# Two modulation units beside w_out's products, and modulation weights loaded two steps ahead, in a two-layer diffusion block

## The chip, the cores and the metric

The kernel runs on one core of a Trainium2 chip. The metric is the time of one execution on the device in microseconds (us), the median over runs. A core has TensorE (matrix products, called PE in the profile), VectorE (DVE), ScalarE (ACT), GpSimd (POOL) and SyncE (SP, which issues most copies from memory). Each engine works through its own queue in order.

## The reference

Two layers over 512 latent tokens `x` and 256 context tokens `ctx`, each of width 1024, all in float32. Each layer first makes six modulation vectors from a conditioning vector, for the latents and for the context:

```
mod_x = split(silu(c) @ w_mod[i] + b_mod[i], 6)
mod_c = split(silu(c_ctx) @ w_mod[i] + b_mod[i], 6)
...
z = modulate(x, norm1_gain[i], mod_x[0], mod_x[1]) @ w_in[i]
x = x + mod_x[2] * mixer_merge(z, attention, ...)        # ends in a product with w_out
x = x + mod_x[5] * swiglu(modulate(x, norm2_gain[i], mod_x[3], mod_x[4]), w_ffn_in[i], w_ffn_out[i])
```

`mixer_merge` adds three gated branches (pooling, windowed attention, spatial gating) and multiplies by `w_out`. The context goes through the same layer in layer 0 and gives only keys and values in layer 1. The output is the latent stream after a last norm.

## The kernel before, in words

**Products.** Every float32 weight is split in a rounded part (`wh`, ScalarE) and a rest (`wl`, VectorE), activations likewise, and each product is three TensorE passes (lines 334 to 336). A raw weight is copied into one of six buffers named `raw` (pool `rawp`, half a megabyte each); the split reads it, and the buffer is free again.

**Modulation.** The product with `w_mod` has a single row on the left, so it is not done on TensorE. `mod_steps` takes a *unit* of 512 of the 6144 columns: four copies `wm` of two 128-row blocks each, and for each block a multiply-add into the accumulator `mac0` for the latents (line 264, VectorE) and, where the context needs it (all of layer 0, units 0 to 3 of layer 1), a multiply on ScalarE (line 261) and an addition into `mac1` on GpSimd (line 262). Then 16 small TensorE products (`ps_mod`, line 274) sum over partitions, and `take_mod` adds the bias. There is one buffer for each accumulator. The copies `wm` use the same six `raw` buffers as the weights. Units 10 and 11 make `mod_x[5]` and `mod_c[5]`, which are first read by the FFN's evictions (line 1238); units 6 to 9 make `mod_x[3]` and `mod_x[4]`.

**Fillers.** `mod_steps` is a generator. The object `fill` holds such generators, and `fill.tick()`, called at chosen places between TensorE's products, takes each one step further; `fill.drain()` runs them to their end. A unit takes five ticks, and a generator two more. Before, each step loads the copy of the next step. The order on an engine is settled when the kernel is built; program order is its priority, and an instruction whose data and buffers are ready may come before earlier ones.

**Stages, with their times in the profile.** The context's mixer of layer 0 (to about 260 us, with units 4 and 5, a step every five ticks), the latents' mixer of layer 0 (to 702 us, the last 55 of them w_out's products, in which `last_first` does the last three output tiles in two halves of the tokens so that the FFN's norm can begin), the first FFN for both streams (702 to 1240 us), the latents' mixer of layer 1 (to about 1690 us) and the second FFN.

**The first FFN** (`Seven`, `ffn_seven`) forms its up products by a scheme with seven products instead of eight for each pair of hidden tiles. `Seven.pair` makes one pair: `load` copies the two raw weights `raw_g` and `raw_u`, `sums` makes sums of their blocks on VectorE, four items `a` to `d` split them and multiply. Pairs 0 to 2 are "early": `seven.ahead` holds their `load` and the first two of their sums, (3, 1), to be called by hand. Between the pairs, after hidden tiles 3, 6, 10, 14 and 18, stand down products: `chunk` multiplies the last 3 or 4 hidden tiles with `w_ffn_out`, two output tiles to an item, into one of two PSUM buffers, and VectorE evicts them into `X` (line 1238). Units 0 to 3 of layer 1 run there, one tick after each pair's item `d`.

Of the kernel before, what the change touches and what calls it, by code (L numbers as in the profile page):

```python
# [5 lines left out]

# [15 lines left out]
KT = D // P  # L22
# [28 lines left out]
def hybrid_dit_kernel(ctx, tc, I, out):  # L51
# [39 lines left out]
    SX = Stream("x", CTX, SEQ, 0)  # L91
# [144 lines left out]

    def mod_steps(l, u0, u1, stride=1):

        nxt = None

        def load(u, k2):
            raw = rawp.tile([P, 2, 512], F32, tag="raw", name=f"wm{l}{u}{k2}")
            nc.sync.dma_start(raw, I["w_mod"][l, k2 * P:(k2 + 2) * P, u * 512:(u + 1) * 512].rearrange("(k p) n -> p k n", p=P))
            return raw

        for u in range(u0, u1):
            nv = 2 if l == 0 or u < 4 else 1
            acc = [macp.tile([P, 512], F32, tag=f"mac{r}", name=f"mac{l}{u}{r}") for r in range(nv)]
            for k2 in range(0, KT, 2):
                if nxt is None:  # L250
                    nxt = load(u, k2)
                    yield
                raw = nxt
                for r, a in enumerate(acc):
                    for k in range(2):
                        sck = scv[:, k2 + k, r:r + 1]
                        if k2 + k == 0:
                            (G if r else V).tensor_scalar(a, raw[:, k, :], sck, None, ALU.mult)
                        elif r:
                            q = t2(f"mq{l}{u}{k2}{k}")  # L260
                            S.activation(q, raw[:, k, :], AF.Copy, scale=sck)  # L261
                            G.tensor_tensor(a, a, q, ALU.add)  # L262
                        else:
                            V.scalar_tensor_tensor(a, raw[:, k, :], sck, a, ALU.mult, ALU.add)  # L264
                if k2 + 2 < KT or u + 1 < u1:
                    nxt = load(u, k2 + 2) if k2 + 2 < KT else load(u + 1, 0)
                for _ in range(stride):
                    yield
            yield
            ps = pmain(f"ps_mod{l}{u}")[:, :P]  # L270
            for r, a in enumerate(acc):
                av = a.rearrange("p (t j c) -> p j t c", j=4, c=32)
                for j in range(4):
                    T_.matmul(ps[32 * j:32 * j + 32, :].rearrange("p (t c) -> p t c", c=32), pick[:, r, :], av[:, j],
                              start=(r == 0), stop=(r == nv - 1))
            take_mod(l, 4 * u, 4, ps, nv)
# [485 lines left out]
                summed = g, a, w  # L762
            yield

    def mixer(s, l, H, L, mods=None, mid=None, then=None, end=None, done=None, last=None):
        nm0 = f"{l}{s.name}"
        rot = s.r == 0
        per = 2048 // s.T
# [111 lines left out]
            fill.tick()  # L880
        if last is not None:
            last(one, acc)
        fill.drain()
        return acc

    def up_units(l, j, w):
# [138 lines left out]
    class Seven:  # L1025
# [71 lines left out]
        def pair(self, j, A, early=None):  # L1097
# [113 lines left out]
            def run_d(w):  # L1211
                self.product(d["P"], w, 0, "T4", False)
                H, L = A(j)
                for i, (x, y) in enumerate(((d["P"], d["g1"]), (d["m5"], d["m6"]))):
                    V.tensor_tensor(y, x, y, ALU.mult)
                    y3 = y.rearrange("p (b t) -> p b t", t=P)
                    S.activation(blocks(H, i), y3, AF.Copy)
                    V.tensor_tensor(blocks(L, i), y3, blocks(H, i).bitcast(F32), ALU.subtract)
                fill.tick()

            if early is not None:
                self.ahead.append((load, partial(sums, (3, 1))))
# [2 lines left out]
    def ffn_seven(sv, streams, l, finish, mods):  # L1225
        fo = I["w_ffn_out"][l]
        heads = [0, 3, 6, 10, 14, 18]
        A = []

        def hidden(j):  # L1230
            t = (sv.fap if j % 6 < 4 else sv.fbp).tile([P, 2, NT], F32R, tag="fa", name=f"fa{l}{j}")
            A.append([t[:, 0, :], t[:, 1, :]])
            return A[j]

        def down(s, n, w, c0, m, ps):
            gemm(ps, w, m, *[[A[c0 + j][x][:, s.cols] for j in range(m)] for x in range(2)])
            x = X[:, n, s.cols]
            V.scalar_tensor_tensor(x, ps, modv[l][:, 40 + n, s.r:s.r + 1], x, ALU.mult, ALU.add)  # L1238

        def size(c0):  # L1240
            return ([h for h in heads if h > c0] + [NF])[0] - c0

        def chunk(c0):
            m = size(c0)
            for n in range(0, KT, 2):
                def prep(n=n):
                    raw = rawp.tile([P, m, 256], F32, tag="raw", name=f"raw_fo{l}{c0}{n}")
                    nc.sync.dma_start(raw, fo[c0 * P:(c0 + m) * P, n * P:(n + 2) * P].rearrange("(k p) n -> p k n", p=P))
                    return split_unit(raw, m, 256, f"fo{l}{c0}{n}")

                def go(w, n=n):
                    for i in range(2):
                        ps = ps_s.tile([P, 1024], F32, tag="ps", name=f"pfo{l}{c0}{n + i}")
                        for s in streams:
                            o = 512 if s.r else 0
                            down(s, n + i, [x[:, :, i * P:(i + 1) * P] for x in w], c0, m, ps[:, o:o + s.T])

                yield prep, go

        sv.hidden = hidden  # L1260

        def items():
            p = sv.first
            for j, x in ((0, 0), (1, 0), (2, 0), (0, 1), (1, 1), (0, 2), (1, 2), (0, 3), (1, 3), (2, 1), (2, 2), (2, 3)):
                yield p[j][x]
            for m in mods:
                fill.add(m)
            for j in range(3, NF):
                yield from sv.pair(j, hidden)
                if j in heads:  # L1270
                    yield from chunk(heads[heads.index(j) - 1])

        def end():
            c0 = heads[-1]
            m = size(c0)
            ou = units(fo[c0 * P:(c0 + m) * P, :], m, f"fo{l}{c0}")
            ws = []

            def one(s, n):
                while len(ws) <= n:  # L1280
                    ws.append(next(ou))
                down(s, n, ws[n], c0, m, pmain(f"pfo{l}{s.name}{c0}{n}")[:, :s.T])

            finish(one)

        return Pipeline(items(), 2), end


# [43 lines left out]
    def last_first(one, acc):  # L1332

        S.activation(warm, ones, AF.Silu)
        for i in range(2):
# [4 lines left out]
            for n in range(KT - 3, KT):  # L1340
                one(n, st, part)
                fill.tick()
                if i:
                    steps(n0, {KT - 3: 2, KT - 2: 4, KT - 1: 3}[n])
                    if n == KT - 3:
                        for load, _ in seven.ahead:
                            load()
                    else:
                        seven.ahead[n - KT + 2][1]()
            if i == 0:  # L1350
                close("att", "kkp")
                seven.fap = zone("fap", 4, "right")
# [12 lines left out]
                T_.matmul(ps[:, b:b + 1], ap, ones[:, 0:1], start=(a == 0), stop=(a == 1))  # L1365
        ssh[i] = ps[:, :2]

    mixer(SX, 0, *hs["x"], mods=mod_steps(0, 6, 12), last=last_first)
    close("act")
    seven.cbp = zone("cbp", 7)  # L1370
    seven.fbp = zone("fbp", 2, "right")
# [33 lines left out]
    steps(cm, 2)  # L1405
    pipe.fill(1)
    next(cm)
    seven.ahead[2][1]()
    pipe.fill(2)
    for _, g in seven.late:  # L1410
        g()
    pipe.go()
    next(cm)
    pipe.fill(2)
    next(cm)
    pipe.go()
    pipe.fill(2)
# [175 lines left out]
```

## Time and profile before

| | |
|---|---|
| median of 3 runs | 2070.0 us (2067.01 to 2070.88) |
| the profiled execution | 2074.72 us |
| its span, first to last instruction | 2072.9 us |
| TensorE busy | 1987.8 us, 96% of the span |
| VectorE, ScalarE, GpSimd busy | 1283.1, 842.1, 435.5 us |
| copied from memory | 225.30 MB, 110 GB/s over the span |
| mean granted clock of TensorE | 0.984 |

The profile is of one execution. A time is counted from the span's first instruction. An engine's busy time is the union of its instructions; the granted clock is 1.00 at 2.4 GHz and 0.50 at 1.2 GHz, its two levels.

### The profile page before, as it was taken

Reading aid. Unit: us, or ns where it says so; the run is one execution under the profiler, and the core shown is the slowest. Engines: PE = TensorE matmul, PEld = TensorE weight load, DVE = VectorE, ACT = ScalarE, POOL = GpSimd, SP = SyncE. Lnnn points to the kernel's source line nnn. Section 1 sums busy time; section 2 is a strip of 40 time slices with the busy share of each in tenths; the row PEclk is TensorE's granted clock in tenths of the full one; section 3 lists DMA queues with packets and bytes.
Section 4 is the critical chain, followed back from the end, with each engine's and each line's share of the span. In section 5 each row is a group of like instructions: output and inputs, shape, how many; then the busy total and the mean of one; then the engine's idle time right before and its main releaser. Section 6 shows DMA issues by size and latency. Waiting matters only on the chain.

```text
span 2072.9 us, 28923 instructions
## 1 busy us (share of the span) xinstructions
PE 1987.8 (96%) x11423; PEld 1719.2 (83%) x11423; DVE 1283.1 (62%) x2018; ACT 842.1 (41%) x1437; POOL 435.5 (21%) x353
## 2 busy tenths in 40 slices
PE   6998999999989899999999999999999999999998
PEld 5898988777767898898998997787778788888887
DVE  4778637675786686675856555776656663334435
ACT  4656434344444563352524345443422343222223
POOL 3436302022764210110101032301211240000000
PEclk8999999999999999999999999999999999999999
DMA  9755643131554132232313233424136643333321
GB/s 302 215 167 155 193 119 94 51 108 51 176 168 135 31 92 77 81 98 72 112 52 112 61 93 102 107 62 127 51 105 214 180 122 102 93 101 92 101 92 41
DMA packets 326728, 233.48 MB, mean 113 GB/s; under 512 B 7680, under 2 KB 300720, under 8 KB 326592
## 3 DMA queue, kind: packets, MB, share of 16 engines
q1 hardware_dynamic: 323072, 226.78, 36.8%
q0 software_dynamic: 3280, 4.76, 1.2%
q8 instruction: 90, 1.47, 0.3%
q14 instruction: 46, 0.38, 0.1%
q10 hardware_dynamic: 240, 0.08, 0.0%
HBM read 225.30 MB, written 2.10 MB: 110 GB/s over the span
## 4 chain that ended last, share of the span: by engine, by line
PE 79%; DVE 11%; issue 3%; ACT 3%; DMA 2%; POOL 2%; ACTq 0%; POOLq 0%; DVEq 0%
PE pP L1093 3%; PE pP L1094 3%; PE pP L1095 3%; PE pfo L334 2%; PE pfo L335 2%; PE pfo L336 2%; PE pfg1x L336 2%; PE pfu1x L335 2%; PE pfu1x L334 2%; PE pfu1x L336 2%; PE pfg1x L335 2%; PE pfg1x L334 2%; PE pg1x L334 2%; PE pg1x L335 2%; PE pg1x L336 2%
## 5 line engine op out<-in xcount | busy, mean ns | idle before, releaser
L262 POOL TENSOR_TENSOR mac<-mac,mq 128x512 f32<-128x512 f32 x84 | 129.2, 1538 | 348.4 <-ACT mq L261 344.3
L264 DVE SCALAR_TENSOR_TENSOR mac<-wm,scv,mac 128x512 f32<-128x512 f32 x140 | 130.7, 934 | 9.9 <-DMA wm<-in_w_mod_dram 7.7
L334 PE MATMUL pfo<-fa,wh_fo 128*128 128x512 f32 (+1 forms) x288 | 100.1, 349 | 9.4 <-DVE X L1238 9.2
L335 PE MATMUL pfo<-fa,wl_fo 128*128 128x512 f32 (+1 forms) x288 | 97.9, 340 | 0.0
L336 PE MATMUL pfo<-fa,wh_fo 128*128 128x512 f32 (+1 forms) x288 | 97.7, 340 | 0.0
L1238 DVE SCALAR_TENSOR_TENSOR X<-pfo,modv,X 128x256 f32<-128x256 f32 (+1 forms) x80 | 48.1, 614 | 72.0 <-PE pfo L336 71.7
L316 ACT ACTIVATE wh_fo<-raw_fo 128x1024 fp32r<-128x1024 f32 (+1 forms) x44 | 44.9, 1020 | 106.8 <-issue 84.1
L317 DVE TENSOR_TENSOR wl_fo<-raw_fo,wh_fo 128x1024 fp32r<-128x1024 f32 (+1 forms) x44 | 54.6, 1240 | 51.1 <-ACT wh_fo L316 51.1
L373 POOL TENSOR_TENSOR rs_fin<-v_fin,half_neg 128x1 f32<-128x1 f32 x4 | 2.9, 722 | 355.8 <-DVE v_fin L371 355.8
L334 PE MATMUL pg0x<-n1x0h,wh_g0x 128*128 128x512 f32 x192 | 75.6, 394 | 1.3 <-ACT tg0x L825 1.3
L335 PE MATMUL pg0x<-n1x0h,wl_g0x 128*128 128x512 f32 x192 | 75.4, 393 | 1.4 <-DVE wl_g0x L317 1.4
L334 PE MATMUL pg1x<-n1x1h,wh_g1x 128*128 128x512 f32 x192 | 75.8, 395 | 0.0
L335 PE MATMUL pg1x<-n1x1h,wl_g1x 128*128 128x512 f32 x192 | 75.6, 394 | 0.0
L336 PE MATMUL pg1x<-n1x1l,wh_g1x 128*128 128x512 f32 x192 | 75.3, 392 | 0.0
L336 PE MATMUL pg0x<-n1x0l,wh_g0x 128*128 128x512 f32 x192 | 74.9, 390 | 0.0
L334 PE MATMUL pfg1x<-n2x1h,wh_fg 128*128 128x512 f32 (+1 forms) x184 | 70.6, 383 | 0.8 <-ACT n2x1h L403 0.8
L334 PEld LDWEIGHTS pfo<-fa,wh_fo 128*128 128x128 f32 x288 | 55.1, 191 | 18.9 <-DVE X L1238 12.1
L336 PE MATMUL pfg1x<-n2x1l,wh_fg 128*128 128x512 f32 (+1 forms) x184 | 70.3, 382 | 0.4 <-POOL n2x1l L404 0.3
L335 PE MATMUL pfu1x<-n2x1h,wl_fu 128*128 128x512 f32 (+1 forms) x184 | 70.2, 382 | 0.0
L336 PE MATMUL pfu1x<-n2x1l,wh_fu 128*128 128x512 f32 (+1 forms) x184 | 70.2, 382 | 0.0
L334 PE MATMUL pfu1x<-n2x1h,wh_fu 128*128 128x512 f32 (+1 forms) x184 | 70.2, 382 | 0.0
L335 PE MATMUL pfg1x<-n2x1h,wl_fg 128*128 128x512 f32 (+1 forms) x184 | 70.1, 381 | 0.0
(803 smaller groups left out, 6592.9 us busy)
## 6 DMA issues: line engine op xcount, KB each, us to landing
wm<-in_w_mod_dram SPq DMA_DIRECT2D x96, 512.0 KB, 4.5
raw_fo<-in_w_ffn_out_dram SPq DMA_DIRECT2D x36, 512.0 KB, 3.4
raw_g0c<-in_w_in_dram SPq DMA_DIRECT2D x24, 512.0 KB, 4.3
raw_g0x<-in_w_in_dram SPq DMA_DIRECT2D x24, 512.0 KB, 4.0
raw_g1x<-in_w_in_dram SPq DMA_DIRECT2D x24, 512.0 KB, 4.4
raw_g<-in_w_ffn_in_dram SPq DMA_DIRECT2D x22, 512.0 KB, 4.1
raw_u<-in_w_ffn_in_dram SPq DMA_DIRECT2D x22, 512.0 KB, 4.5
raw_fg<-in_w_ffn_in_dram SPq DMA_DIRECT2D x22, 512.0 KB, 3.9
```

Source lines behind the costliest of these rows:

```text
L262: G.tensor_tensor(a, a, q, ALU.add)
L264: V.scalar_tensor_tensor(a, raw[:, k, :], sck, a, ALU.mult, ALU.add)
L316: S.activation(wh, raw_ap, AF.Copy)
L317: (eng or V).tensor_tensor(wl, raw_ap, wh.bitcast(F32), ALU.subtract)
L334: T_.matmul(ps, wh, H, start=first, stop=False)
L335: T_.matmul(ps, wl, H, start=False, stop=False)
L336: T_.matmul(ps, wh, L, start=False, stop=last)
L373: G.tensor_tensor(rs, v, half_neg[:, :nb], ALU.pow)
L1093: T_.matmul(ps, wh[:, k0 + k, :], H, start=first and k == 0, stop=False, skip_group_check=True)
L1094: T_.matmul(ps, wl[:, k0 + k, :], H, start=False, stop=False, skip_group_check=True)
L1095: T_.matmul(ps, wh[:, k0 + k, :], L, start=False, stop=k == 3, skip_group_check=True)
L1238: V.scalar_tensor_tensor(x, ps, modv[l][:, 40 + n, s.r:s.r + 1], x, ALU.mult, ALU.add)
```

## The change

`mod_steps` keeps a queue of loaded copies: the first step loads two, each later step takes the oldest and loads one more, across the ends of units. In layer 0's latent mixer the filler makes units 6 to 9 only; units 10 and 11 are added before w_out's products, and what is left of them (the last `ps_mod` and its bias) is not drained there but before the fillers of the first FFN begin. In the first FFN the tick after each pair's item `d` is gone; ticks stand after the second output tile of each item of a down chunk, and after both of the third item, five to a chunk. The early sums: those of pair 0 stay in w_out's products, those of pair 1 go to where those of pair 2 stood, and those of pair 2 one step further.

```diff
--- before.py
+++ after.py
@@ -2,7 +2,7 @@
 from collections import deque
 from contextlib import ExitStack
 from functools import partial
-from itertools import chain
+from itertools import chain, islice
 
 import concourse.bass as bass
 import concourse.tile as tile
@@ -236,7 +236,8 @@
 
     def mod_steps(l, u0, u1, stride=1):
 
-        nxt = None
+        nxt = deque()
+        todo = iter([(u, k2) for u in range(u0, u1) for k2 in range(0, KT, 2)])
 
         def load(u, k2):
             raw = rawp.tile([P, 2, 512], F32, tag="raw", name=f"wm{l}{u}{k2}")
@@ -247,10 +248,10 @@
             nv = 2 if l == 0 or u < 4 else 1
             acc = [macp.tile([P, 512], F32, tag=f"mac{r}", name=f"mac{l}{u}{r}") for r in range(nv)]
             for k2 in range(0, KT, 2):
-                if nxt is None:
-                    nxt = load(u, k2)
+                if not nxt:
+                    nxt.extend(load(*s) for s in islice(todo, 2))
                     yield
-                raw = nxt
+                raw = nxt.popleft()
                 for r, a in enumerate(acc):
                     for k in range(2):
                         sck = scv[:, k2 + k, r:r + 1]
@@ -262,8 +263,7 @@
                             G.tensor_tensor(a, a, q, ALU.add)
                         else:
                             V.scalar_tensor_tensor(a, raw[:, k, :], sck, a, ALU.mult, ALU.add)
-                if k2 + 2 < KT or u + 1 < u1:
-                    nxt = load(u, k2 + 2) if k2 + 2 < KT else load(u + 1, 0)
+                nxt.extend(load(*s) for s in islice(todo, 1))
                 for _ in range(stride):
                     yield
             yield
@@ -762,7 +762,7 @@
                 summed = g, a, w
             yield
 
-    def mixer(s, l, H, L, mods=None, mid=None, then=None, end=None, done=None, last=None):
+    def mixer(s, l, H, L, mods=None, mid=None, then=None, end=None, done=None, last=None, keep=False):
         nm0 = f"{l}{s.name}"
         rot = s.r == 0
         per = 2048 // s.T
@@ -880,7 +880,8 @@
             fill.tick()
         if last is not None:
             last(one, acc)
-        fill.drain()
+        if not keep:
+            fill.drain()
         return acc
 
     def up_units(l, j, w):
@@ -1216,7 +1217,6 @@
                     y3 = y.rearrange("p (b t) -> p b t", t=P)
                     S.activation(blocks(H, i), y3, AF.Copy)
                     V.tensor_tensor(blocks(L, i), y3, blocks(H, i).bitcast(F32), ALU.subtract)
-                fill.tick()
 
             if early is not None:
                 self.ahead.append((load, partial(sums, (3, 1))))
@@ -1254,6 +1254,8 @@
                         for s in streams:
                             o = 512 if s.r else 0
                             down(s, n + i, [x[:, :, i * P:(i + 1) * P] for x in w], c0, m, ps[:, o:o + s.T])
+                        if i or n == 4:
+                            fill.tick()
 
                 yield prep, go
 
@@ -1263,6 +1265,7 @@
             p = sv.first
             for j, x in ((0, 0), (1, 0), (2, 0), (0, 1), (1, 1), (0, 2), (1, 2), (0, 3), (1, 3), (2, 1), (2, 2), (2, 3)):
                 yield p[j][x]
+            fill.drain()
             for m in mods:
                 fill.add(m)
             for j in range(3, NF):
@@ -1345,8 +1348,8 @@
                     if n == KT - 3:
                         for load, _ in seven.ahead:
                             load()
-                    else:
-                        seven.ahead[n - KT + 2][1]()
+                    elif n == KT - 2:
+                        seven.ahead[0][1]()
             if i == 0:
                 close("att", "kkp")
                 seven.fap = zone("fap", 4, "right")
@@ -1365,7 +1368,7 @@
                 T_.matmul(ps[:, b:b + 1], ap, ones[:, 0:1], start=(a == 0), stop=(a == 1))
         ssh[i] = ps[:, :2]
 
-    mixer(SX, 0, *hs["x"], mods=mod_steps(0, 6, 12), last=last_first)
+    mixer(SX, 0, *hs["x"], mods=mod_steps(0, 6, 10), end=lambda: fill.add(mod_steps(0, 10, 12)), last=last_first, keep=True)
     close("act")
     seven.cbp = zone("cbp", 7)
     seven.fbp = zone("fbp", 2, "right")
@@ -1405,13 +1408,14 @@
     steps(cm, 2)
     pipe.fill(1)
     next(cm)
-    seven.ahead[2][1]()
+    seven.ahead[1][1]()
     pipe.fill(2)
     for _, g in seven.late:
         g()
     pipe.go()
     next(cm)
     pipe.fill(2)
+    seven.ahead[2][1]()
     next(cm)
     pipe.go()
     pipe.fill(2)
```

## Rows read from the trace of the kernel before

**Rows 1.** The page: an engine line, a group of additions, a group of copies.

```profile
PE 1987.8 (96%) x11423; PEld 1719.2 (83%) x11423; DVE 1283.1 (62%) x2018; ACT 842.1 (41%) x1437; POOL 435.5 (21%) x353
...
L262 POOL TENSOR_TENSOR mac<-mac,mq 128x512 f32<-128x512 f32 x84 | 129.2, 1538 | 348.4 <-ACT mq L261 344.3
...
wm<-in_w_mod_dram SPq DMA_DIRECT2D x96, 512.0 KB, 4.5
```

**Rows 2.** Waits: engine and tile, released by whom: total us, times, longest.

```profile
PE pfo L334 <- DVE X L1238: 9.2, 7, 2.9
...
PE pb0x L335 <- DVE wl_b0x L317: 5.4, 1, 5.4
...
PE s1x L547 <- ACT pr1x L560: 3.5, 1, 3.5
...
PE pg0x L334 <- ACT tg0x L825: 1.3, 1, 1.3
...
ACT wh_g0x L316 <- DMA raw_g0x<-in_w_in_dram: 17.0, 7, 4.6
```

**Rows 3.** Stretches: length, busy time by engine (instructions), clock, copy share, GB/s.

```profile
590.00:646.00 56.00, 49.29 (x242) 39.00 (x242) 40.60 (x41) 23.26 (x33) 33.79 (x21) 0.94 0.54 160
646.00:702.00 56.00, 54.84 (x316) 48.18 (x314) 27.33 (x42) 20.92 (x34) 16.51 (x12) 1.00 0.29 85
702.00:745.00 43.00, 36.18 (x170) 33.85 (x171) 39.38 (x54) 28.16 (x48) 4.49 (x1) 0.84 0.09 25
...
776.00:805.00 29.00, 27.51 (x154) 23.86 (x154) 18.72 (x32) 4.79 (x8) 0.00 (x0) 1.00 0.24 67
...
1127.00:1171.00 44.00, 41.12 (x230) 35.53 (x219) 25.22 (x41) 7.18 (x11) 3.31 (x2) 0.92 0.17 49
...
1420.00:1462.00 42.00, 38.14 (x208) 30.62 (x207) 29.18 (x54) 15.20 (x30) 4.69 (x6) 0.96 0.50 137
```

**Rows 4.** Timeline of VectorE, mixer's end: start, us, instruction, count [idle before <-releaser].

```profile
594.60 1.23 DVE L317 TENSOR_TENSOR wl_g0x<-raw_g0x,wh_g0x 128x1024 fp32r<-128x1024 f32 x1 [4.12 <-ACT wh_g0x L316]
...
596.57 1.52 DVE L258 TENSOR_SCALAR mac<-wm,scv 128x512 f32<-128x512 f32 x1
...
599.19 0.74 DVE L264 SCALAR_TENSOR_TENSOR mac<-wm,scv,mac 128x512 f32<-128x512 f32 x1
...
601.64 7.53 DVE L264 SCALAR_TENSOR_TENSOR mac<-wm,scv,mac 128x512 f32<-128x512 f32 x6
...
609.68 1.22 DVE L317 TENSOR_TENSOR wl_b0x<-raw_b0x,wh_b0x 128x1024 fp32r<-128x1024 f32 x1
```

**Rows 5.** Timeline of VectorE, the first instruction of unit 11.

```profile
622.38 0.49 DVE L258 TENSOR_SCALAR mac<-wm,scv 128x512 f32<-128x512 f32 x1 [2.58 <-PE ps_mod L274]
```

**Rows 6.** Timeline of VectorE, the same chunk start.

```profile
1129.74 1.24 DVE L209 TENSOR_TENSOR modv<-mT,colsB 128x8 f32<-128x8 f32 x1
1130.91 0.74 DVE L264 SCALAR_TENSOR_TENSOR mac<-wm,scv,mac 128x512 f32<-128x512 f32 x1
```

**Rows 7.** Timeline of VectorE, two splits at an earlier chunk start.

```profile
936.22 1.82 DVE L317 TENSOR_TENSOR wl_fo<-raw_fo,wh_fo 128x1024 fp32r<-128x1024 f32 x1 [0.58 <-ACT wh_fo L316]
...
938.90 1.22 DVE L317 TENSOR_TENSOR wl_fo<-raw_fo,wh_fo 128x1024 fp32r<-128x1024 f32 x1
```

**Rows 8.** Timeline of VectorE, end of w_out: first and last of three gaps; a sum.

```profile
690.94 0.48 DVE L865 SCALAR_TENSOR_TENSOR X<-po0x_0xe,modv,X 128x256 f32<-128x256 f32 x1 [2.40 <-PE po0x_0xe L336]
...
694.69 0.48 DVE L865 SCALAR_TENSOR_TENSOR X<-po0x_0xo,modv,X 128x256 f32<-128x256 f32 x1 [1.73 <-PE po0x_0xo L336]
...
703.18 0.69 DVE L1114 TENSOR_TENSOR S<-raw_g,raw_u 128x512 f32<-128x512 f32 x1
```

**Rows 9.** Timeline of VectorE, layer 1's attention.

```profile
1444.19 1.54 DVE L264 SCALAR_TENSOR_TENSOR mac<-wm,scv,mac 128x512 f32<-128x512 f32 x2 [4.44 <-DMA wm<-in_w_mod_dram]
```

**Rows 10.** Timeline of TensorE, the first product after the split at 594.60.

```profile
599.73 0.39 PE L334 MATMUL pg0x<-n1x0h,wh_g0x 128*128 128x512 f32 x1
```

**Rows 11.** Groups by form, 500 to 660 us: count, busy us, mean ns, idle before.

```profile
L264 DVE SCALAR_TENSOR_TENSOR mac<-wm,scv,mac 128x512 f32<-128x512 f32 x35 | 44.7, 1276 | 0.6
```

## The prediction

> **What bounds the kernel now.** I read the page first. TensorE is busy for 1987.8 of 2072.9 us [rows 1], so nothing the other engines do counts unless it leaves TensorE waiting or its clock low; all that can be won is in its idle 85 us. So the next view is the list of TensorE's waits [rows 2], kept to the stretches that the diff touches: 5.4 us in one wait of layer 0's mixer for the split `wl_b0x`, 1.3 us there for `tg0x`, 9.2 us in seven waits of the first FFN's down products for an eviction into `X`, 3.5 us in layer 1's attention for `pr1x`. The third view is the table by stretches, with the granted clock [rows 3]. Where a long wait falls, the mean clock is under 1.00: some microseconds after it ran at 1.2 instead of 2.4 GHz. What that loses is (1 - clock) times the stretch: 0.06 x 56 = 3.4 us at the mixer's end, 0.08 x 44 = 3.5 us in the last down chunk of the loop, 0.04 x 42 = 1.7 us in layer 1's attention. The timelines of VectorE then tell what stood ahead of the late instruction.
>
> **Part 1, two units leave the mixer's end.** From 596.57 us VectorE runs the eight multiply-adds of unit 10: 1.52 + 0.74 + six in 7.53 = 9.8 us, and only then, at 609.68, the split that TensorE waits for [rows 4]. Why in one piece? A unit's accumulator is a single buffer: unit 11's first instruction waits 2.58 us for TensorE's `ps_mod`, which reads unit 10's [rows 5]. Unit 10's weights have landed by the time that the accumulator comes free, so its additions follow each other at once, whatever ticks they were given to. In the new kernel units 10 and 11 are not in the mixer: its last ticks carry nothing. The wait, the clock behind it and the wait at `tg0x` go: 5.4 + 3.4 + 1.3 = 10.1 us. The ends are nothing (another split comes late there) and 10.1; I take 10.1, since no other wait of this stretch is over 0.3 us once the additions are gone.
>
> **Part 2, the first FFN's ticks move from the pairs into the down chunks.** At the start of the last chunk, where TensorE has the longest of the seven waits, 2.9 us [rows 2], VectorE runs 1.24 + 0.74 = 2.0 us and more of unit 3's work [rows 6], ahead of the evictions. The new ticks begin after a chunk's second output tile, so this work stands later: 2.9 us and the 3.5 us of clock go. Three other chunk starts hold a split that a GpSimd addition stretches, 1.82 us at 936.22 where the next one takes 1.22 [rows 7]: 0.6 x 3 = 1.8 us. Together 8.2 us; the ends are 0 and the 9.2 + 3.5 = 12.7 us of all these waits.
> What takes their place: four units, one to a chunk. A unit costs VectorE 9.8 us beside GpSimd. In a chunk of three hidden tiles VectorE is free for 29 - 18.7 = 10.3 us [rows 3], which just holds it; chunks of four are longer. TensorE has two buffers to be evicted, and behind each pair of additions wait the next evictions. I charge 1 us to each of four chunks, 4 us; the ends are 0 (free time suffices) and four times the worst chunk, 4 x 6.4 = 26 us. A row nearer to the low end decides: the additions that already lie in the chunk of 776 to 805 us do so at full clock.
>
> **Part 3, the two units in w_out's products.** VectorE is busy 27.3 of 56 us there, GpSimd 16.5 [rows 3], so unit 10 is covered. Unit 11 can't start before unit 10's accumulator is read, at the seventh tick, near 688 us. Its 9.8 us of additions then have three idle gaps of VectorE between 688.5 and 694.7 us to fill, 2.40 to 1.73 us, 5.5 in all [rows 8]; 4.3 us are left over, in front of the normalisation that the first FFN enters with. From 702 to 745 us VectorE is busy 39.4 of 43 us and TensorE only 36.2: what is added there shows. Against it, the sums of pair 1 (two of 0.69 us [rows 8]) leave the place just before `wl_sg`: -1.4 us. Their new place comes after the first combinations, where those of pair 2 stood, and pair 2's go one step on: the same work in the same busy stretch, nothing. GpSimd makes 8 additions of 1.54 us each [rows 1], with the `rs_n2h` of the norm queued behind one of them: 1.5 us. Sum 4.3 - 1.4 + 1.5 = 4.4, and I take 4 us; the ends are 0, if the additions run early, and 9.8 + 3.4 = 13 us, if none is hidden and one more low stretch of the clock follows. The last `ps_mod` and its bias are drained before the fifth of the pairs' late items, far from their first reader, at no cost. The eight copies of 512 KB that go past w_out's on SyncE's queue add some 4 MB to a stretch at 85 GB/s, hidden, since TensorE is not waiting for copies there.
>
> **Part 4, loads two steps ahead, in all units.** The same copies are issued one step earlier; each holds one of the six `raw` buffers longer. What it can remove is one wait: at 1444.19 us VectorE stands 4.44 us for a `wm` copy [rows 9], and the softmax behind it leaves TensorE waiting 3.5 us and then 1.7 us worth of clock. That copy was waiting for a buffer, so issuing it earlier may only make another one late. Ends 0 and 5.2 us: I take the middle, 2.6. What it costs: weights get their buffer later. In layer 0's mixer a split that starts at 594.60 and takes 1.23 us [rows 4] is used from 599.73 on [rows 10], 3.9 us of cover, so a shift under that costs nothing. In the context's mixer, with ticks five apart, two buffers of six stand waiting for long; I charge 1 us, between 0 and one landing plus a low clock, 4.5 + 3.4 = 7.9 us.
>
> **Sum:** -10.1 - 8.2 + 4 + 4 - 2.6 + 1 = -11.9 us. The profiled execution took 2074.72 us, 4.7 us above the median of 2070.0; -11.9 gives 2062.8 on its scale and 2058 on the median's.
>
> **A rule that speaks against part 3.** GpSimd's additions slow VectorE's: an addition takes 0.74 us alone [rows 6] and 1.28 us on average in the stretch where GpSimd adds too [rows 11]. The Trainium skill, "SBUF — State Buffer", section "Who interferes with whom", says that VectorE and GpSimd share one port pair as an exclusive lock, that a VectorE instruction with two SBUF inputs contends with a GpSimd one that reads SBUF, and that whichever starts later waits for the whole of the other. The trace agrees in kind. By it, in chunks only splits and additions suffer and the evictions don't, as in part 2; at the FFN's entry, where nearly all of VectorE's work has two SBUF inputs, the 8 x 1.54 = 12.3 us of GpSimd additions would be paid almost whole, and the sum would be -11.9 + 8.3 = -3.6 us. A like result, priced from rows alone, is the first rival.
>
> **Rivals.** (B) Unit 11 stands unhidden before the FFN: 13 us in place of 4, so -11.9 + 9 = -2.9, 2067 us. For it: VectorE full from 702 us on; against: 5.5 us idle just before. (C) The change does not do what it says: the additions follow the accumulator and the landing, not the tick, so with loads earlier they come in one piece elsewhere; the 10.1 us and half of part 2's 8.2 stay: +2.3, 2072 us. For it: a piece of that kind at 596 us [rows 4]; against: the units' places past the mixer's end are fixed by their loads. (D) Slower: weights are starved of `raw` buffers in the three mixers that carry units. It decides when a weight copy comes more than 3.9 us later. Then each of three stretches loses a landing, 4.5 us [rows 1], and a low stretch of the clock, 3.4: 3 x 7.9 = 23.7, less the 1 charged: +10.8, 2081 us. For it: the splits' first halves already wait 17.0 us in all, seven times, for a copy to land [rows 2]; against: one step more in one of six buffers.
>
> **Numbers.** Forecast 0.61, B 0.13, C 0.13, D 0.13. A measurement of this kernel can tell about 0.2%, 4.1 us, from no change. Faster than 2065.9 us: nearly all of the forecast, a third of B, a little of C: 0.64. Within: 0.19. Slower than 2074.1: D and the upper part of C: 0.17. Low end: all gains at their upper ends, 10.1 + 12.7 + 5.2 = 28, less 3 of cost: 2045. High end: past C and short of D, 2075; outside lie most of D and little else.
>
> **What would show it.** Right: no wait of 5 us and clock 1.00 from 590 us to the mixer's end; chunk starts waiting under 1.5 us; the eight additions of a unit inside each of four chunks; no `wm` wait on VectorE in layer 1. Wrong: TensorE idle for more than 11 us between w_out's last products and the first combinations; waits for `X` in the middle of chunks; waits on splits whose copy landed late.

## The result, and the profile after

The changed kernel takes 2082.87 us (median of 4 runs, 2082.55 to 2085.41) against 2069.07 for the kernel before in the same comparison: a ratio of 1.0065, 95% interval 1.0051 to 1.0079. It is slower by about 0.65%; the forecast was 2058. Its profiled execution took 2085.41 us with a span of 2083.0, 10.1 more than the profiled one of before; those 10.1 us are what follows. By the medians the change costs 13.8 us. The profiled execution of before lay 4.7 us above its median, that of the change 2.5 us, so differences between the two profiles come out some 3 us too small, and which stage holds them is not shown.

The page of the changed kernel: the engine line and two groups, whose rows of before are in [rows 1] or unchanged in kind. (Its line numbers are up to three higher than before's.)

```profile
PE 1991.1 (96%) x11423; PEld 1723.7 (83%) x11423; DVE 1277.0 (61%) x2018; ACT 842.8 (40%) x1437; POOL 420.8 (20%) x353
...
L263 POOL TENSOR_TENSOR mac<-mac,mq 128x512 f32<-128x512 f32 x84 | 126.0, 1500 | 74.3 <-ACT mq L262 70.0
```

The amount of work is the same and VectorE and GpSimd are even a little less busy. So the next view is TensorE's waits, as in [rows 2]:

```profile
PE pfo L334 <- DVE X L1238: 21.5, 15, 3.3
...
PE ps_ssh L1368 <- ACT sqxo L867: 4.0, 1, 4.0
...
PE pg0x L335 <- DVE wl_g0x L317: 3.8, 1, 3.8
PE ps_mod L274 <- POOL mac L263: 3.4, 1, 3.4
```

The waits for `wl_b0x` (5.4) and for `pr1x` (3.5) are gone, as forecast. The waits for an eviction into `X` have grown from 9.2 to 21.5 us, and three waits of 3.4 to 4.0 us are new. The stretches, as in [rows 3], show what each does to the clock:

```profile
779.40:814.60 35.20, 29.90 (x153) 25.48 (x152) 23.89 (x32) 8.41 (x13) 9.62 (x6) 0.90 0.33 99
948.70:993.20 44.50, 39.19 (x218) 33.28 (x218) 29.13 (x40) 9.46 (x14) 12.60 (x8) 0.92 0.29 84
590.00:640.00 50.00, 50.00 (x235) 40.98 (x234) 31.57 (x32) 16.57 (x22) 15.24 (x10) 1.00 0.38 112
640.00:711.00 71.00, 60.35 (x342) 52.40 (x341) 41.01 (x57) 31.83 (x53) 35.96 (x27) 0.93 0.42 122
```

The first two are down chunks 1 and 3 of the first FFN (the five chunks of the loop are numbered in order of time; the fifth, the prediction's last, holds no unit now). The same two chunks before:

```profile
776.00:804.80 28.80, 27.31 (x153) 23.66 (x153) 18.60 (x31) 4.73 (x7) 0.00 (x0) 1.00 0.24 67
936.90:974.20 37.30, 35.78 (x202) 31.14 (x201) 18.84 (x29) 5.33 (x7) 0.05 (x1) 1.00 0.20 56
```

Chunk 1 took 28.8 us before at clock 1.00 and takes 35.2 at 0.90. The third stretch is the mixer's end: TensorE is busy for all of it. The fourth runs from there through w_out into the FFN's entry: TensorE is idle for 71.00 - 60.35 = 10.6 us of it. Cutting the span at the start of the first product of each stage, and at the first and last products of the chunks, on TensorE's timeline of both traces:

| stage | before | after | difference |
|---|---|---|---|
| start to the 13th of the 24 output tiles `pg0x` of layer 0's latent mixer (538 us) | 538.1 | 538.2 | +0.1 |
| from there, four output tiles | 38.5 | 43.8 | +5.3 |
| rest of that mixer, to w_out | 78.1 | 66.1 | -12.0 |
| w_out and FFN entry, to the first down chunk | 121.3 | 131.3 | +10.0 |
| down chunks 1 to 4 | 132.6 | 159.0 | +26.4 |
| pairs between them, last chunk, rest of the first FFN | 340.2 | 328.3 | -11.9 |
| layer 1 | 824.1 | 816.3 | -7.8 |

Three gains of 31.7 us stand against three losses of 41.7. The largest loss is 6.4, 5.6, 7.2 and 7.2 us in the four chunks that now hold a unit. In chunk 3 TensorE is idle for 44.50 - 39.19 = 5.3 us in place of 37.30 - 35.78 = 1.5, and loses (1 - 0.92) x 44.5 = 3.6 us of clock: 3.8 + 3.6 = 7.4 us, against 7.2 measured. VectorE's timeline in it shows what the evictions into `X` (L1238) stand behind:

```profile
953.63 2.45 DVE L265 SCALAR_TENSOR_TENSOR mac<-wm,scv,mac 128x512 f32<-128x512 f32 x2
956.00 1.79 DVE L1115 TENSOR_TENSOR S<-raw_g,raw_u 128x512 f32<-128x512 f32 x1
957.71 0.74 DVE L1238 SCALAR_TENSOR_TENSOR X<-pfo,modv,X 128x512 f32<-128x512 f32 x1
958.37 1.11 DVE L1117 TENSOR_TENSOR raw_u<-raw_u 128x512 f32<-128x512 f32 x1
959.41 3.44 DVE L265 SCALAR_TENSOR_TENSOR mac<-wm,scv,mac 128x512 f32<-128x512 f32 x2
962.77 0.74 DVE L1238 SCALAR_TENSOR_TENSOR X<-pfo,modv,X 128x512 f32<-128x512 f32 x1
963.43 1.09 DVE L265 SCALAR_TENSOR_TENSOR mac<-wm,scv,mac 128x512 f32<-128x512 f32 x1
964.44 2.30 DVE L317 TENSOR_TENSOR wl_fo<-raw_fo,wh_fo 128x1024 fp32r<-128x1024 f32 x1
966.66 0.86 DVE L1238 SCALAR_TENSOR_TENSOR X<-pfo,modv,X 128x256 f32<-128x256 f32 x2
```

GpSimd's and TensorE's timelines of the same time:

```profile
954.16 11.50 POOL L263 TENSOR_TENSOR mac<-mac,mq 128x512 f32<-128x512 f32 x7
```

```profile
963.56 0.39 PE L334 MATMUL pfo<-fa,wh_fo 128*128 128x256 f32 x1 [3.30 <-DVE X L1238]
...
967.19 0.79 PE L334 MATMUL pfo<-fa,wh_fo 128*128 128x512 f32 x1 [1.47 <-DVE X L1238]
967.78 0.63 PE L335 MATMUL pfo<-fa,wl_fo 128*128 128x512 f32 x1
```

While GpSimd adds for 11.5 us, a sum of 0.69 us takes 1.79, two additions of 0.74 take 3.44, a split of 1.22 takes 2.30. The evictions themselves keep their 0.74 us; they stand in line. TensorE waits 3.30 us for the one at 962.77, and from 964.5 to 971.4 us it runs at 1.2 GHz (0.63 us for a product of 0.39).

The new wait in layer 0's mixer, on SyncE's queue and on ScalarE:

```profile
530.88 0.37 SPq L328 DMA_DIRECT2D raw_g0x<-in_w_in_dram  x1
534.33 0.37 SPq L244 DMA_DIRECT2D wm<-in_w_mod_dram  x1
542.36 0.37 SPq L328 DMA_DIRECT2D raw_g0x<-in_w_in_dram  x1
```

```profile
546.49 1.06 ACT L316 ACTIVATE wh_g0x<-raw_g0x 128x1024 fp32r<-128x1024 f32 x1 [6.59 <-DMA raw_g0x<-in_w_in_dram]
```

The copy `wm` of 534.33 takes a buffer of `raw`; the next weight copy is issued 8 us later, right after a split (which ends at 542.33) frees one. Before, that weight copy was issued at 533.21. In w_out TensorE waits for unit 10's sum over partitions:

```profile
686.77 0.43 PE L274 MATMUL ps_mod<-mac,pick 128*32 128x128 f32 x8 [3.42 <-POOL mac L263]
```

Weights are late here too: w_out's last weight copy is issued 28 us after its first product, and 20 us after it in the kernel wout_only below, which loads one step ahead and has no such wait. ScalarE's multiplies stand in its queue behind the splits of these weights, and GpSimd's additions behind the multiplies. From 688.1 us on TensorE runs at 1.2 GHz for 3.4 us. And at the FFN's entry VectorE's evictions stand behind instructions that GpSimd stretches, a sum from 0.69 us to 1.75 for one, and ScalarE's square, for which TensorE waits 4.0 us, behind the eviction:

```profile
696.47 1.02 DVE L1056 TENSOR_TENSOR th<-X,ps_rbh 128x384 f32<-128x384 f32 x2 [0.21 <-PE ps_rbh L1050]
697.40 1.15 DVE L1062 TENSOR_SCALAR th<-th,A,modv 128x256 f32<-128x256 f32 x1
...
702.57 1.75 DVE L1115 TENSOR_TENSOR S<-raw_g,raw_u 128x512 f32<-128x512 f32 x1
704.24 0.54 DVE L1056 TENSOR_TENSOR th<-X,ps_rbh 128x384 f32<-128x384 f32 x1
704.71 1.29 DVE L1117 TENSOR_TENSOR raw_u<-raw_u 128x512 f32<-128x512 f32 x1
705.92 0.47 DVE L865 SCALAR_TENSOR_TENSOR X<-po0x_0xo,modv,X 128x256 f32<-128x256 f32 x1
```

### The profile page after: what moved, and what is told of

Read it like the earlier page. It is cut to its first block, busy times and chain, and to the rows that moved or that the text cites. A ratio compares the mean times of both kernels' runs of the same rounds, so it can differ in the third digit from the quotient of the medians.

```text
span 2083.0 us, 28911 instructions
## 1 busy us (share of the span) xinstructions
PE 1991.1 (96%) x11423; PEld 1723.7 (83%) x11423; DVE 1277.0 (61%) x2018; ACT 842.8 (40%) x1437; POOL 420.8 (20%) x353
## 4 chain that ended last, share of the span: by engine, by line
PE 56%; DVE 6%; issue 2%; ACT 1%; DMA 1%; POOL 1%; POOLq 0%; ACTq 0%; DVEq 0%
PE pP L1095 3%; PE pP L1094 3%; PE pP L1096 3%; PE pfo L334 2%; PE pfg1x L336 2%; PE pfu1x L335 2%; PE pfu1x L334 2%; PE pfu1x L336 2%; PE pfg1x L334 2%; PE pfg1x L335 2%; PE pg1x L334 2%; PE pfo L335 2%; PE pfo L336 2%; PE pg1x L335 2%; PE pg1x L336 2%; PE pfo1x L336 2%
## 5 line engine op out<-in xcount | busy, mean ns | idle before, releaser
L334 PE MATMUL pfo<-fa,wh_fo 128*128 128x512 f32 (+1 forms) x288 | 103.1, 360 | 21.5 <-DVE X L1238 21.5
L336 PE MATMUL pfo<-fa,wh_fo 128*128 128x512 f32 (+1 forms) x288 | 100.0, 348 | 0.0
L1238 DVE SCALAR_TENSOR_TENSOR X<-pfo,modv,X 128x256 f32<-128x256 f32 (+1 forms) x80 | 47.9, 612 | 64.1 <-PE pfo L336 64.0
L259 POOL TENSOR_SCALAR mac<-wm,scv 128x512 f32<-128x512 f32 x12 | 20.6, 1716 | 309.7 <-ACT mq L262 146.8
```

Of the source, the lines that this page charges most:

```text
L334: T_.matmul(ps, wh, H, start=first, stop=False)
L336: T_.matmul(ps, wh, L, start=False, stop=last)
```

## The experiments

Twelve kernels; the time before was 2069.3 to 2071.1 us beside them. All of them cut into the same stages (us, from the profiled execution; "mixer" from 538 us to w_out, "entry" from there to the first chunk):

| kernel | median | ratio, 95% | mixer | entry | chunks | rest of FFN | layer 1 |
|---|---|---|---|---|---|---|---|
| before | | 1 | 116.7 | 121.3 | 132.6 | 340.2 | 824.1 |
| the change | 2082.9 | 1.0065 (1.0051-1.0079) | 110.0 | 131.3 | 159.0 | 328.3 | 816.3 |
| loads_only | 2075.2 | 1.0021 (1.0012-1.0031) | 122.7 | 120.4 | 134.7 | 339.7 | 817.7 |
| chunks_only | 2080.1 | 1.0048 (1.0036-1.0061) | 116.6 | 121.2 | 152.8 | 328.1 | 823.2 |
| wout_only | 2065.2 | 0.9974 (0.9963-0.9986) | 104.8 | 126.5 | 132.9 | 338.8 | 824.4 |
| no_chunks | 2069.7 | 0.9995 (0.9986-1.0004) | 110.0 | 129.5 | 134.3 | 340.8 | 819.9 |
| no_gpsimd | 2049.8 | 0.9898 (0.9880-0.9916) | 108.7 | 120.9 | 134.9 | 328.3 | 818.9 |
| act_only | 2051.6 | 0.9906 (0.9894-0.9919) | 110.7 | 125.5 | 133.8 | 328.3 | 816.6 |
| vec_after | 2050.9 | 0.9903 (0.9890-0.9916) | 108.7 | 127.6 | 133.2 | 327.1 | 818.8 |
| wout_l1 | 2060.0 | 0.9949 (0.9935-0.9962) | 104.6 | 124.7 | 132.8 | 340.1 | 818.0 |
| mix1 | 2069.2 | 0.9993 (0.9985-1.0002) | 104.6 | 132.0 | 131.5 | 343.7 | 818.6 |
| vec_pairs | 2057.7 | 0.9935 (0.9923-0.9947) | 104.6 | 126.2 | 132.6 | 334.5 | 816.4 |
| best | 2047.7 | 0.9896 (0.9882-0.9909) | 104.7 | 126.7 | 135.0 | 327.1 | 816.4 |
| vec_all | 2051.8 | 0.9915 (0.9901-0.9930) | 107.1 | 127.0 | 133.0 | 327.0 | 818.4 |

Stages of one execution scatter by about 2 us: wout_only and wout_l1 have the same program up to the first chunk and differ by 1.8 at the entry. The time to the 13th `pg0x` tile, not in the table, is 535.3 to 538.6 us in the seven kernels that have the same program there. So stages show where a large difference lies, and whole kernels are compared by their medians. In vec_all the 13th tile's first product runs 2.5 us ahead of its turn, while another product waits for its split; its mixer is counted from 8.2 us after the 12th tile's start, where that product stands in the others.

**The parts, one by one.** Two theories stood for the loss. T: the chunks lose because a unit's additions stand in front of the evictions. D: weights come late because two `wm` copies wait in `raw` (rival D of the prediction). Three kernels do one part of the change on the kernel before, a fourth undoes the ticks alone.

loads_only has the new `mod_steps` and nothing else:

```diff
-                    nxt = load(u, k2)
+                    nxt.extend(load(*s) for s in islice(todo, 2))
...
+                nxt.extend(load(*s) for s in islice(todo, 1))
```

> The kernel before with only the loads two steps ahead. Theory T (the loss lies in the down chunks, where a unit's eight additions stand in one piece in front of the evictions): this part costs nothing in the first FFN; layer 1's attention loses its wait for a modulation copy, -7 us, and the new wait of layer 0's mixer at 542 us comes with it, +5, then the old one at 611 us stays: 2067 us, 0.999. Theory D (weights starved of raw buffers by the second copy in flight): slower by 8 us or more, with waits on splits whose copy landed late.

chunks_only moves the ticks and nothing else:

```diff
-                fill.tick()
...
+                        if i or n == 4:
+                            fill.tick()
```

> The kernel before with only the first FFN's ticks moved into the down chunks, loads one step ahead. Theory T: the first FFN is 10 to 18 us longer, 2083 us, 1.007, with waits for X in the middle of four chunks. Theory D: the chunk ticks alone cost nothing, the pairs gain: 2062 us, 0.996.

wout_only has units 10 and 11 in w_out and the sums later:

```diff
-    mixer(SX, 0, *hs["x"], mods=mod_steps(0, 6, 12), last=last_first)
+    mixer(SX, 0, *hs["x"], mods=mod_steps(0, 6, 10), end=lambda: fill.add(mod_steps(0, 10, 12)), last=last_first, keep=True)
...
```

> The kernel before with only units 10 and 11 in w_out's products and the early sums later, loads one step ahead. Theory T: the mixer's end gains the 10 us of the wait at 611 us and its clock, the entry of the first FFN loses the same 10 us to unit 11 after the seventh tick: 2070 us, 1.000. If the entry's loss came from copies issued earlier (D), the gain alone is left: 2060 us, 0.995.

no_chunks is the changed kernel with the ticks back behind item `d`:

```diff
+                fill.tick()
...
-                        if i or n == 4:
-                            fill.tick()
```

> The changed kernel with the first FFN's ticks back behind the pairs. Theory T: the 14.5 us that the trace of the changed kernel shows between the first chunk and layer 1 come back: 2068 us against 2069 of before, 1.000. Theory D: the loads stay as they are, so most of the loss stays: 2080 us, 1.005.

The ticks alone, with loads one step ahead, cost 20.2 us in the chunks (132.6 to 152.8) and win 12.1 between them: for the chunks T stands, and D has no more than a share (2.1 us in loads_only alone, and 26.4 - 20.2 = 6.2 where both come together). The loads alone cost 6 us in layer 0's mixer and win 6.4 in layer 1, yet the median is 4.9 us above before's; the stages of the one profile don't show where those lie. The two units in w_out are a gain by themselves: 11.9 won in the mixer, 5.2 paid at the entry, a time between the two theories' forecasts. no_chunks is back at the time of before, as T said. But it differs from wout_l1, below, in nothing but loads two ahead outside layer 1's mixer, and is 9.7 us slower (2069.7 against 2060.0). By stages it is 5.4 longer in layer 0's mixer (110.0 against 104.6) and 4.8 at the entry, where `ps_mod` waits 2.7 us in no_chunks and 0.2 in wout_l1. So D is right in one of the three mixers that it named, w_out's products with it.

**What stretches the chunks.** T says that the additions are in the way, not why 9.8 us of them cost 26. Theory G: GpSimd's additions stretch VectorE's. Theory O: VectorE's own additions are enough. no_gpsimd takes the context's share of six units (10 and 11, and layer 1's 0 to 3) out of the changed kernel; everything on VectorE stays.

```diff
-            acc = [macp.tile([P, 512], F32, tag=f"mac{r}", name=f"mac{l}{u}{r}") for r in range(nv)]
+            acc = [macp.tile([P, 512], F32, tag=f"mac{r}", name=f"mac{l}{u}{r}") for r in range(1 if l or u >= 10 else nv)]
...
-            for r, a in enumerate(acc):
+            for r, a in enumerate(acc * 2 if nv > len(acc) else acc):
```

> The changed kernel, with the context's share of six units left out (units 10 and 11 of layer 0, units 0 to 3 of layer 1): no multiply on ScalarE and no addition on GpSimd for them; the context's modulation of these units is taken from the latents' sums, so part of the computation is missing. VectorE's additions, the ticks, the copies and all TensorE products stay. Theory G (in the chunks and at the entry GpSimd's additions stretch every VectorE instruction with two SBUF inputs beside them, and the evictions into X stand behind those): the chunks cost 1 to 2 us each in place of 6.6, that is 18 to 22 us less, and the stretch from w_out to the first chunk loses 4 us in place of 10; together 2082.9 - 26 = 2057 us, ratio to before 0.993 to 0.996. Theory O (VectorE's own eight additions in front of the evictions are enough): the chunks still cost 5 us or more each, at most 6 us are won in all, 2077 us, ratio 1.003 or more.

The chunks fall from 159.0 to 134.9 and the entry from 131.3 to 120.9. VectorE's timeline in the same chunk, same instructions in the same order as above:

```profile
928.12 1.54 DVE L265 SCALAR_TENSOR_TENSOR mac<-wm,scv,mac 128x512 f32<-128x512 f32 x2
930.61 0.69 DVE L1115 TENSOR_TENSOR S<-raw_g,raw_u 128x512 f32<-128x512 f32 x1 [0.96 <-DMA raw_u<-in_w_ffn_in_dram]
931.22 0.75 DVE L1238 SCALAR_TENSOR_TENSOR X<-pfo,modv,X 128x512 f32<-128x512 f32 x1
931.88 0.69 DVE L1117 TENSOR_TENSOR raw_u<-raw_u 128x512 f32<-128x512 f32 x1
932.48 1.53 DVE L265 SCALAR_TENSOR_TENSOR mac<-wm,scv,mac 128x512 f32<-128x512 f32 x2
933.93 0.74 DVE L1238 SCALAR_TENSOR_TENSOR X<-pfo,modv,X 128x512 f32<-128x512 f32 x1
934.59 0.74 DVE L265 SCALAR_TENSOR_TENSOR mac<-wm,scv,mac 128x512 f32<-128x512 f32 x1
935.25 1.22 DVE L317 TENSOR_TENSOR wl_fo<-raw_fo,wh_fo 128x1024 fp32r<-128x1024 f32 x1
936.38 0.87 DVE L1238 SCALAR_TENSOR_TENSOR X<-pfo,modv,X 128x256 f32<-128x256 f32 x2
```

From the first addition here to the last eviction it is 13.9 us in the changed kernel and 9.1 here, for the same instructions. O falls. But no_gpsimd left out ScalarE's multiplies too. act_only keeps them and leaves out seven of a unit's eight GpSimd additions:

```diff
-                            G.tensor_tensor(a, a, q, ALU.add)
+                            if not (l or u >= 10):
+                                G.tensor_tensor(a, a, q, ALU.add)
```

> The changed kernel with seven of GpSimd's eight additions of each of six units left out (layer 0's 10 and 11, layer 1's 0 to 3); ScalarE's multiplies for them stay, and the context's modulation of these units is wrong by the missing terms. Theory G (GpSimd's additions are the cost): within 3 us of the kernel that leaves ScalarE's multiplies out too, 2050 to 2053 us, ratio 0.990 to 0.9915. Rival A (the multiplies, which stand before the splits in ScalarE's queue, are a good part of it): 2065 us or more.

The chunks take 133.8: the multiplies cost nothing there. At the entry 125.5 against 120.9: there ScalarE's queue does count.

vec_after asks the question from the other side. It leaves nothing out; the context's share is made on VectorE, eight more multiply-adds a unit:

```diff
+                        own = r and l == 0 and u < 10
-                            (G if r else V).tensor_scalar(a, raw[:, k, :], sck, None, ALU.mult)
+                            (G if own else V).tensor_scalar(a, raw[:, k, :], sck, None, ALU.mult)
-                        elif r:
+                        elif own:
```

> The changed kernel with the context's share of the same six units made by multiply-adds on VectorE, eight more of 0.74 us a unit, in place of ScalarE's multiplies and GpSimd's additions; nothing is left out. Theory G: an addition costs VectorE 0.74 us again and nothing else is stretched; a unit is 16 x 0.74 = 11.8 us, in a chunk of three tiles 1.5 us more than VectorE has free, in one of four less than it has. Chunks cost 2 to 3 us each in place of 6.6, the way from w_out to the first chunk 6 in place of 10: 2082.9 - 15 - 4 = 2064 us, ratio 0.997. Rival O (VectorE's own time is what the chunks lack): 6 us more of it in each of four chunks and at the entry make it slower than the change, over 2085 us, 1.007.

It is 32 us faster than the change, more than G expected, with more work on the engine that was late. The stretch of chunk 3, first of no_gpsimd, then of vec_after (columns as in [rows 3]):

```profile
923.20:961.00 37.80, 36.53 (x217) 31.45 (x217) 23.45 (x39) 5.17 (x7) 0.00 (x0) 1.00 0.34 98
```

```profile
929.50:966.70 37.20, 36.76 (x222) 32.01 (x221) 28.17 (x47) 5.16 (x7) 0.00 (x0) 1.00 0.33 100
```

VectorE is busy for 28.2 of 37.2 us there, a larger share than the 29.1 of 44.5 in the changed kernel, at full clock. A busy share does not tell whether evictions are late; what stands ahead of each one does.

**Versions.** wout_l1 is wout_only with loads two steps ahead in layer 1's mixer alone (`deep` is 1 there and 0 elsewhere):

```diff
+        deep = l == 1 and u0 >= 4
...
+                    nxt.extend(load(*s) for s in islice(todo, 1 + deep))
```

> The kernel before with units 10 and 11 in w_out and the sums later, and with loads two steps ahead in the units of layer 1's mixer (4 to 11) alone; ticks of the first FFN as before. If loads two ahead pay only where a copy was late, at 1444 us of the kernel before, and cost only in layer 0's mixer, where the new wait at 541 us stands: 5 to 7 us under the 0.9974 of the units alone, 2059 us, ratio 0.9945. Rival: the copies of layer 1 take buffers from that layer's weights as they did in layer 0, and the sum is nothing: 2065 us, 0.997.

It came out as expected: the gain in layer 1 stays (6.1), and there is no loss in layer 0's mixer (104.6 against wout_only's 104.8). mix1 adds two more edits:

```diff
+            if keep:
+                fill.tick()
...
+                if j in (4, 7, 11, 15, 19):
+                    fill.tick()
...
+                if j not in (3, 6, 10, 14, 18):
+                    fill.tick()
```

> The same kernel as the one with loads two ahead in layer 1 alone, with two more edits: two ticks in place of one after each of w_out's first five output tiles, so that unit 11 starts before the last three tiles; and in the first FFN the tick of the five pairs that stand before a down chunk goes to item b of the pair behind it. If a unit's additions go where its ticks are: the entry to the FFN loses 1 us in place of 5, and the chunk starts give back 6 to 8 of the 9.2 us of waits for X: 2059 - 4 - 7 = 2048 us, ratio 0.990. Rival (additions follow the accumulator and the landings, not the ticks): within 2 us of the kernel without the two edits, 0.9945.

A miss: 9 us slower than wout_l1. TensorE's waits in it:

```profile
PE pP L1097 <- ACT m L1190: 7.7, 6, 1.7
...
PE ps_mod L275 <- DVE mac L266: 4.2, 1, 4.2
...
PE ps_mod L275 <- POOL mac L264: 3.8, 2, 2.0
```

Earlier ticks put `ps_mod` earlier in TensorE's queue, and there it stands until the unit's last addition is done: 8.0 us of waits, the entry 7.3 longer. In the FFN the waits for `X` fell (6.2 in all) and waits for ScalarE's `m`, behind the unit's multiplies, took their place.

vec_pairs is wout_l1 with VectorE's additions of vec_after.

> The kernel with units 10 and 11 in w_out, the ticks of the first FFN behind the pairs and loads two ahead in layer 1's mixer alone (2060.0 us), with the context's share of units 10 and 11 and of layer 1's 0 to 3 on VectorE. Theory G: the first FFN wins the 3 to 6 us by which the pairs ran shorter with no GpSimd additions at all, less 1 for the longer queue of VectorE, and the entry 1 to 2: 2055 us, ratio 0.9925. Rival: the pairs hid GpSimd's additions already, and 35 us more on VectorE make splits late: 2060 to 2066 us.

It is 2.3 us faster than wout_l1, with intervals that overlap. In its profile, of an execution 3.0 us under its median, the pairs gain 5.6; that they, too, paid for GpSimd is likely and not settled. The chunk ticks without GpSimd gain more (327.1 against 334.5). best is the changed kernel with VectorE's additions in layer 1's units and loads two ahead in layer 1 alone; vec_all has them in layer 0's units too.

```diff
+                    nxt.extend(load(*s) for s in islice(todo, 1 + l))
...
+                        own = r and l == 0
...
```

> The changed kernel with two edits: the context's share of layer 1's units 0 to 3 on VectorE (units of layer 0 keep ScalarE and GpSimd), and loads two steps ahead in layer 1 alone, one step in layer 0. If the stages add up: layer 0's mixer and the way to the first chunk as in the kernel with loads two ahead in layer 1 alone (first chunk 8.9 us earlier than before), the first FFN as with VectorE's additions (11.0 us shorter than before), layer 1's attention 5 to 7 us shorter: 2070.7 - 8.9 - 11.0 - 6 = 2045 us, ratio 0.9875. Rival: with loads one step ahead in layer 0 the copies of units 10 and 11 come later, the entry takes back 3 us or more: 2048 us or over.

> The same kernel with the context's share of all units on VectorE, those of layer 0 too; GpSimd makes no addition of a unit any more. Theory G, where it holds in the mixers as well: splits and additions of the two mixers of layer 0 are no longer stretched, 0 to 3 us there, and the entry's additions by GpSimd, 4 us, are replaced by 11.8 us more of VectorE: 2044 to 2050 us, ratio 0.987 to 0.990. Rival: in the mixers VectorE, busy for 39 of 56 us, is what the splits wait for, and 4 units x 6 us more show there: 2055 us or more.

best has the lowest median, 1.04% under before. It stayed 2.7 us over its forecast and just under its rival's 2048; the entry took 126.7 and the chunks 135.0 where wout_l1 had 124.7 and vec_after 133.2, each about within the scatter. Its interval overlaps that of vec_after, so the last 3 us between them are not settled. vec_all is 4 us above it in the median, with intervals that overlap a little, between its own forecast and its rival. Its mixer is 2.4 us longer (107.1 against 104.7), little more than the scatter: that VectorE has no room for eight more additions a unit there is not shown.

## Why the prediction was wrong

- **Part 1** held: no wait, clock 1.00; 12.0 us for 10.1. Some 1.1 us of the rest are the two units' `ps_mod` products, which moved to w_out with them.
- **Part 2, the gain** held: 11.9 for 8.2, inside its ends.
- **Part 2, the cost, is the step that failed:** "I charge 1 us to each of four chunks, 4 us". It measured 26.4, at the upper end of 26; 20.2 where nothing but the ticks was moved (chunks_only). The low end was chosen by the row of the chunk of 776 to 805 us, where additions run at full clock. But that row also reads POOL 0.00 [rows 3], and of a unit's eight instructions on VectorE the chunk held two:

```profile
789.57 1.54 DVE L264 SCALAR_TENSOR_TENSOR mac<-wm,scv,mac 128x512 f32<-128x512 f32 x2 [0.19 <-DMA wm<-in_w_mod_dram]
```

  With none of GpSimd's additions in it, it was nearer to vec_after (0.6 us in all four chunks) than to the change. The row that bore on the change was the split of 1.82 us beside a GpSimd addition [rows 7], which I priced as a cost that the change removes and not as one that it brings into chunks. And "9.8 us beside GpSimd" against "10.3 us" free left out that splits and sums of the chunk are stretched as well, and that the evictions stand behind them all.
- **Part 3** measured 10.0 for 4, within its ends of 0 to 13. By itself, with loads one step ahead, the move cost 5.2 (wout_only) or 3.4 (wout_l1). The rest came with the loads, which part 4 priced without w_out: the wait of 3.4 us for `ps_mod`, and 3.4 us at 1.2 GHz behind it, half of which is lost. Both kernels without GpSimd's additions lack that wait: no_gpsimd gives back all of the 10, act_only, which keeps ScalarE's multiplies, 5.8. vec_after pays 6.3: with VectorE nearly full there, the work costs wherever it is done.
- **Part 4**: layer 1's attention, from its first `py1x` to its first `ps_a1x` product, fell from 98.2 to 92.8 us, and to 92.8 in every kernel that loads two ahead there: 5.4 for 2.6, at the upper end of 5.2; the wait went and no other took its place. The cost was put at the wrong mixer. In layer 0's latent mixer I had "a shift under that costs nothing", under 3.9 us; the weight copy was issued 9 us later, and 5.3 us were lost. The context's mixer lost nothing that shows for the 1 charged.
- **Sum:** -12.0 + 5.3 + 10.0 + 26.4 - 11.9 - 5.4 - 2.3 for the rest, within the scatter, = +10.1 us, where I had -11.9. Of the 22 us between, 22.4 are the chunks; what the loads cost and what the gains came out higher cancel.
- **Rivals.** D's time, 2081, is near the result, for another reason in the main: its mechanism made 5.3 us in the mixer and about half of the entry's 10.0, nothing that shows in the two other mixers. B's cost, 13 us unhidden at the entry, came near (10.0) but was a side matter. The 10.1 us went, so C fell. The sign named for "wrong", waits for `X` in the middle of chunks, is what the trace showed.
- **The rule.** The Trainium skill, "SBUF — State Buffer", section "Who interferes with whom": the trace agrees with it in the rows of chunk 3 (two SBUF inputs: 0.69 to 1.79 us; evictions, with one input from PSUM: 0.74 either way). I wrote that by it "in chunks only splits and additions suffer and the evictions don't". That is true of their length and false of their start, in one in-order queue. At the entry I had it that nearly all of VectorE's work has two SBUF inputs, so that 12.3 us would be paid almost whole; without GpSimd's additions the entry is 5.8 us shorter (act_only). The normalisation's `th<-X,ps_rbh` has one input from PSUM and kept its length, 0.54 us with GpSimd beside it and 0.55 without; its TENSOR_SCALAR, 0.40 us at 706.32 with GpSimd idle, took 1.15 beside it at 697.40. The Trainium skill, "GPSIMD Engine Reference", section "Engine selection", puts elementwise work on VectorE and calls GpSimd about twice as slow with two inputs; 1.50 us an addition against VectorE's 0.74 agrees.

## What to carry to other kernels

When work is moved beside a busy engine, take the duration from a row in which the same set of engines is busy, and count what becomes longer around it, not the moved work alone. Before moving additions off VectorE to spare it, try them on VectorE: here 16 short instructions a unit delayed the evictions less than 8 of them with 8 on GpSimd beside. A deeper prefetch out of a shared pool should be set per stage: one step more won 5.4 us where a copy was late and cost 9.7 where weights needed the buffer (no_chunks against wout_l1).

## What was not expected of the hardware

How unevenly the two engines lose: the five additions of VectorE shown in chunk 3 took 7.0 us beside GpSimd and 3.8 without it, one split 2.30 and 1.22, while GpSimd's own additions took 1.64 us each there and 1.28 for one beside which VectorE was nearly idle (at 773.30 us before). And the clock: the waits for `X` in the four chunks, 21 us in all and none over 3.3, came with four stretches at 1.2 GHz of 6.8, 6.8, 6.8 and 3.4 us, up to half of which, 11.9 us, was lost on top.
